# Two normalisation factors spread over the partitions by transfers through memory in place of matmuls

## The chip, the cores and the metric

The kernel runs on one core of one Trainium2 chip. The core has a matrix engine (TensorE, PE in the profile; its weight loads are listed apart as PEld), VectorE (DVE), ScalarE (ACT), GpSimd (POOL) and SyncE (SP), which issues most of the DMA transfers. On-chip data lies in 128 partitions; matmul results go to accumulators in eight banks of their own (PSUM). The metric is the device time of one execution in microseconds, less is better: before the change 732.38 us, the median of three runs (732.17 to 732.54).

## The reference

One block of a hybrid transformer, 512 tokens of width 1024, all in float32. The input is normalised, projected to eleven pieces, and goes through two attention branches whose gated sum is projected back; a squared-ReLU feed-forward layer and a last norm follow.

```python
proj = rmsnorm(h, g_mix) @ w_in
gq, gk, gv, gr, z_gf, z_gb, cq, ckv, kr, z_ma, z_mb = split(proj)
y_gla = gla_branch(gq, gk, gv, gr, z_gf, z_gb, ...)      # gated linear attention, 4 heads
q  = rmsnorm(cq, g_q) @ w_uq                             # latent attention, 8 heads
kv = rmsnorm(ckv, g_kv) @ w_ukv
y_mla = softmax attention of q, k, v with rotary positions
h = h + (sigmoid(z_ma) * y_gla + sigmoid(z_mb) * y_mla) @ w_out
h = h + square(relu(rmsnorm(h, g_mlp) @ w_ff1)) @ w_ff2
return rmsnorm(h, g_final)
```

What matters here is `rmsnorm(cq, g_q)` and `rmsnorm(ckv, g_kv)`: each token's latent (384 features for cq, 256 for ckv) is multiplied by one factor per token, 1 / sqrt(mean of its squares + eps).

## The kernel before

A product in full precision is made of three rounded ones: both operands are split into a rounded part (`h`) and the rest (`l`), and TensorE runs h·h, h·l and l·h into one accumulator (`mm3`). ACT makes the rounded part of a weight, DVE (or POOL) the rest. So one product of 128 features by 512 tokens over the 1024 inputs is 24 matmuls, and its weights pass through DMA (`zb4f`), ACT (`zb4h`) and DVE (`zb4l`) before TensorE can use them.

The program goes through four stretches: the first products with the input (to about 27 us), the big projections gr, za and gv, the four heads of the linear attention (173 to 281 us, with the latents cq and ckv and the gates zb put between as filling), the latent attention with the output projection, and the feed-forward layer.

The projections lie with features on the partitions and tokens along the row. A factor per token is then needed as a row of 512 that is the same in all 128 partitions. The latents' factors begin elsewhere: the sums of squares come out of a matmul with a column of ones (`feature_sums`), which leaves token `p` of block `j` in partition `p`, column `j`, a tile of 128 by 4. Class `Latent` turns these into a row in three steps:

- `sums`: two small DVE instructions and a power on POOL give the factor (`cqr`, `ckvr`).
- `diagonals`: DVE multiplies by `r_x` (the factor of the input's norm), rounds the factor and takes the rest, and multiplies each with the identity, four blocks of 128 by 128 (`cqdg`, `ckvdg`).
- `spread`: two matmuls of a matrix of ones with these diagonals leave the row in all partitions of an accumulator (`cqrs`, `ckvrs`).

`normed` then multiplies the latent's two or three tiles by it on DVE (`cqc`, `ckvc`) and splits them (`cqhl`, `ckvhl`). The up-projections `ro`, `uq`, `uk` and `uv` use the result.

The input's own factor is spread in the same way (`xdg`, `xrs`) in the first stretch. Its squares are summed by ACT from four tiles of the input with tokens on the partitions (`x_rows`, `xr` in the profile).

What sets the order: DVE, ACT, TensorE and POOL run their instructions in the order in which they are written, piece by piece; the part from the last head on is first recorded and then written out by the list `SEQUENCE` (an entry `D:cqc2` is the next DVE instruction that writes a tile cqc2), the last rows by `LAST_ROWS`. A scheduler joins these pieces, and may put the first instructions of the recorded part among the last ones of the part before; it also places the transfers, which SP issues one after the other. `tail`, at the very end, is a row of matmuls of 128 by 64 whose result nobody reads. Tile buffers are taken in turn from pools (26 of the large kind `u4`, four accumulators of the kind `mm`).

Of the kernel before, what the change touches and what calls it, by code (L numbers as in the profile page):

```python
# [11 lines left out]
F32 = mybir.dt.float32  # L12
# [6 lines left out]
P = 128  # L19
S = 512  # L20
# [77 lines left out]
def tile_block(ctx: ExitStack, tc: tile.TileContext, t, out: bass.AP):  # L98
    nc = Held(tc.nc)
    sb = ctx.enter_context(tc.tile_pool(name="sb", bufs=1))  # L100
    pp = ctx.enter_context(tc.tile_pool(name="pp", bufs=4, space=bass.MemoryType.PSUM))

# [200 lines left out]
    def rounded_diagonal(r, name):  # L303
# [3 lines left out]
        return diagonal(rh, rl, name)  # L307

    def diagonal(rh, rl, name):
        diag = u4(f"{name}dg", F32R, (P, 2, NT, P))  # L310
        for x, c in ((0, raw(rh)), (1, rl)):
            nc.vector.tensor_tensor(
                diag[:, x], ident.unsqueeze(1).to_broadcast([P, NT, P]),
                c.unsqueeze(2).to_broadcast([P, NT, P]), op=ALU.mult,
            )
        return diag

    def spread(diag, name, tag="at"):
        rs = ps(tag, f"{name}rs")
        for x in range(2):  # L320
            nc.tensor.matmul(
                rs, ones_r, diag[:, x].rearrange("p a b -> p (a b)"), start=x == 0, stop=x == 1
            )
        return rs
# [172 lines left out]
    x_diag = rounded_diagonal(r_x, "x")  # L497
# [442 lines left out]
    class Latent:  # L940
# [454 lines left out]
    for h in range(GH - 1):  # L1395
# [10 lines left out]
        (rotary.angles, rotary.reduced, cq_.diagonals)[h]()  # L1406
# [49 lines left out]
    ckv_.sums()  # L1456
    zb5 = proj_run(w_b, xT)
# [3 lines left out]
    ckv_.diagonals()  # L1461
# [9 lines left out]
    ckv_.spread()  # L1471
# [394 lines left out]
    def last_rows(ph):  # L1866
# [34 lines left out]
        for _ in range(20):  # L1901
            nc.tensor.matmul(tail[:, : P // 2], ones_r, ones_r[:, : P // 2], start=True, stop=True)
# [106 lines left out]
    for x in range(2):  # L2009
# [4 lines left out]
        S:wr1f P:ckvss*4 D:ckvr D:cqc1 P:kt*4 S:wr1f D:ckvr P:y15*4 A:cqhl1 G:ckvr A:bds P:sc1*5 A:cqhl2 D:sc0 P:y14*4  # L2014
        D:zb4 A:wr0h A:wk0h D:ckvr D:cqhl2 G:wr0l A:wk0h A:qF D:sc1*2 D:cqhl0 A:sc1 S:wk1f D:ckvrh D:ckvdg D:krsin
        D:ckvrl D:ckvdg D:cqhl1 D:sc1 P:zb5*24 A:wr1h D:sc0 A:yg4 D:zb5 G:wr1l A:cos D:kswap A:yg5 G:wk0l S:wq0f
        P:ro0*9 A:kT D:kr P:ckvrs*2 S:wq0f A:wk1h A:wk0h G:wk1l S:wq0f A:sc0 D:roa1 G:qF A:wk0h D:roa0 D:kr P:ro1*9
        G:wk0l D:ckvc0 D:ckvc1 A:ckvhl0 D:ckvhl0 D:kT A:tb5 D:rob1 A:wk1h D:rob0 A:kbuf0 D:roa0 A:ckvhl1 D:kbuf0
        A:wq0h P:zb6*24 A:ro0 D:sc0 G:wq0l D:ro0 G:wk1l S:zb7f P:gla3st*12 A:gla3s D:ckvhl1 G:wk0l P:gla3o1*12 D:roa1
        G:wk0l D:gla3s A:ro1 P:gla3o0*12 D:zb6 S:wq1f D:ro1 S:wq1f S:kbuf1 P:uq0*9 S:q001 S:q000 P:gla3o0*6 A:gla3sq  # L2020
        S:wq1f A:wk1h P:gla3o1*6 A:zb7h S:q000 G:wk1l S:q001 A:gla3sq P:uk0*6 D:zb7l A:gla3sq S:q211 A:q000 S:q110
        A:kbuf0 S:wq2f P:uv01*12 A:kbuf1 D:kbuf0 S:q110 A:gla3sq A:v01 G:gla3ss S:kbuf2 G:gla3ss A:wq1h S:q011 A:wk1h
        G:gla3ss A:q010 G:wq1l S:q010 D:grc D:grb S:q010 D:kbuf1 S:wq2f D:q011 S:w2_10 D:q001 S:wk2f D:grb D:v01
        S:q011 P:zb7*24 D:zb7 S:q211 P:s00*3 D:grc S:q210 P:s01*3 S:w2_20 D:top01 S:w2_30 D:top00 S:wq2f A:e00 P:uq1*9
        A:tb4 P:y17*4 A:q100 P:y16*4 A:e01 P:s03*3 S:q110 D:top03 A:wk2h S:q111 P:s11*3 A:yg6 G:wk2l D:tot00 D:e01
        S:kbuf3 A:e00 G:wk1l D:top11 A:e03 S:q111 P:uk1*6 D:q101 S:bo11f A:kbuf2 P:s02*3 A:wq2h S:q111 A:e11 P:s10*3
        G:wq2l S:bo11f D:top10 S:w2_20 D:top02 A:e10 A:e02 P:uv11*12 P:tp000*4 P:tp001*4 A:wk2h D:tot02 D:kbuf2
        A:pT000 G:wk2l D:tot10 A:tb6 S:kbuf3 D:pT010 P:uv10*12 S:w2_00 A:v10 P:s12*3 A:e02 S:q100 D:top12 A:pT001
        S:q100 D:e03 A:bo11h S:wk3f D:v10 P:uv00*12 S:q101 A:yg7 P:s13*3 P:uq2 D:top13 A:v00 S:kbuf2 A:e10 D:e11
# [12 lines left out]
        A:q300 D:tot40 P:s51*3 P:av2 A:e42 S:q300 D:top51 P:tp310*4 S:q301 D:tb2 A:pT300 S:w2_31 A:e51 D:tot42 D:pT310
        P:uk3*6 S:q311 A:e40 D:e43 S:w2_21 P:s50*3 D:e41 A:q310 G:my1 D:pT311 S:q310 P:tp311*4 A:pT301 P:tp401*4
        D:top50 G:mx1 S:bo20f A:e42 D:pT311 S:w2_31 A:wk3h D:q311 A:kbuf2 G:wk3l A:e50 D:kbuf2 G:yo0 A:pT401 D:tot50
        P:av3*12 D:q301 G:zo1 A:kbuf3 P:tp400*4 D:pT411 G:w2_20 A:pT400 P:tp410*4 A:pT400 P:s61*3 G:w2_11 D:top61
        P:s60*3 G:w2_01 D:top60 A:e61 D:kbuf3 A:e60 P:uv31*12 D:pT410 A:bo50h P:tp411*4 P:av4 D:tb3 A:pT401 P:s62*3
        D:tot60 D:pT410 G:mx1 A:e60 D:top62 G:yo0 D:e51 A:e62 G:my1 P:uv30*12 D:pT411 A:v31 P:s63*3 G:yo1 D:top63
        A:e50 P:s71*3 A:ghyo0 D:e61 G:w2_21 D:top71 A:e63 P:av4*4 G:w2_20 D:bo50l A:e71 P:s70*3 P:tp500*4 A:pT500
        D:tot62 P:tp510*4 S:w2_00 A:v30 D:top70 P:tp600*4 S:h2 A:gao1 D:e63 A:pT500 S:h0 D:pT510 G:gao1 A:pT600 S:h1
        D:v30 P:av4*7 D:pT510 G:yo1 P:wox0*3 D:tb4 P:tp501*4 G:zo0 A:pT501 P:wox1*3 G:glyo0 A:e70 D:pT511 P:s72*3  # L2050
        P:av5 D:pT610 P:tp511*4 G:my2 D:top72 A:pT501 P:s73*3 D:tot70 G:mx2 A:ghyo1 D:pT511 P:av5*2 A:e62 G:zo2 D:e71
        P:tp601*4 A:pT601 G:glyo1 D:v31 A:e72 D:top73 A:e70 P:av5*9 D:pT611 A:e73 P:wox0 P:tp610*4 D:tot72 A:pT600
        D:tb5 P:tp700*4 A:pT700 P:tp701*4 D:pT610 G:my2 P:tp611*4 D:pT710 A:pT601 G:yo2 P:wox1*3 A:e72 D:pT611 G:mx2
# [24 lines left out]
        P:g3x1*12 A:hp2 D:h3 D:hp2 A:junk A:ms2 S:out D:ms2 S:out D:ms3 D:hp3 P:gend*14 P:tail*20 A:junk D:ms3 A:hp3  # L2078
# [122 lines left out]
```

## Time and profile before

| | |
|---|---|
| median of three runs | 732.38 us (732.17 to 732.54) |
| the profiled execution: its time, and its span from the first to the last instruction | 732.09 us, 730.3 us |
| TensorE busy, matmuls | 726.3 us (99%), 4174 |
| DVE, ACT, POOL busy | 619.8 (85%), 498.7 (68%), 225.8 us (31%) |
| TensorE clock granted, mean | 0.999 |
| the four matmuls cqrs and ckvrs | at 241.5 and 265.1 us |

A row of a timeline is: start in us, length in us, engine, line, operation, output <- inputs, the sizes and how many; in brackets what the engine idled for just before, in us. Nearly all instructions have one of two lines: L76 where a list writes them out, L90 elsewhere. The letters f, h and l at the end of a weight's name are its full, rounded and rest copy; numbers of buffers are left out. A matmul's length is the time until its result is out; the next one starts earlier, so that 24 matmuls of 512 columns take about 5.44 us.

### The profile page before, as it was taken

The page shows a single profiled execution, that of the slowest core. Times are in us where ns is not written, and L with a number is a line of the kernel's source. Part 1 is how long each engine was busy: PE and PEld are TensorE (multiplying, and loading weights), DVE is VectorE, ACT ScalarE, POOL GpSimd, SP SyncE. Part 2 cuts the span into 40 slices and gives each one's busy share as a digit, 9 for nine tenths or more (in the row PEclk, how much of TensorE's full clock was granted, in tenths as well). Part 3 has the DMA queues.
Part 4 walks back from the last instruction along what each step waited for, and adds up shares of the span by engine and source line. Part 5 has one row for each costly group of instructions (what it writes and reads, how often), then busy time and mean ns, then how long its engine had stood idle before and what let it go on. Part 6 is the DMA issues. An engine that isn't in the chain of part 4 may idle for free.

```text
span 730.3 us, 11455 instructions
## 1 busy us (share of the span) xinstructions
PE 726.3 (99%) x4174; PEld 641.2 (88%) x4174; DVE 619.8 (85%) x859; ACT 498.7 (68%) x846; POOL 225.8 (31%) x290
## 2 busy tenths in 40 slices
PE   9999999999999999999999999999999999999998
PEld 8888888888888888888888999889988998899987
DVE  6677887889988897789999789998699869987797
ACT  7456565595696864988866889545774477646976
POOL 1842020243843843226763512200111012100224
PEclk9999999999999999999999999999999999999999
DMA  9968683521222324657957899871987088814864
GB/s 323 346 176 198 210 180 88 84 62 29 58 58 59 89 46 110 184 158 189 251 88 208 196 205 201 187 215 57 245 182 201 9 223 206 206 59 134 183 89 143
DMA packets 82777, 112.06 MB, mean 153 GB/s; under 512 B 16384, under 2 KB 35712, under 8 KB 82720
## 3 DMA queue, kind: packets, MB, share of 16 engines
q1 hardware_dynamic: 65344, 77.81, 34.0%
q0 software_dynamic: 17088, 33.30, 27.3%
q8 instruction: 33, 0.54, 0.3%
q10 hardware_dynamic: 288, 0.22, 0.1%
q14 instruction: 24, 0.20, 0.1%
HBM read 106.32 MB, written 2.10 MB: 148 GB/s over the span
## 4 chain that ended last, share of the span: by engine, by line
PE 99%; issue 0%
PE f3x L90 3%; PE f2x L90 3%; PE f1x L90 3%; PE f0x L90 3%; PE first L90 3%; PE s L76 3%; PE av L76 3%; PE wox L76 3%; PE g2x L90 3%; PE g1x L90 3%; PE g0x L90 3%; PE gvx L90 3%; PE zax L90 3%; PE grx L90 3%; PE gk L90 2%; PE cq L90 2%
## 5 line engine op out<-in xcount | busy, mean ns | idle before, releaser
L90 POOL DMA_DIRECT2D w<-in_w_ff x32 | 38.6, 1205 | 240.1 <-DMA w<-in_w_ff 134.8
L76 ACT ACTIVATE e<-s,top 128x512 f32<-128x512 f32 x32 | 21.9, 688 | 8.5 <-DVE top L76 7.4
L76 DVE TENSOR_REDUCE top<-s 128x1 f32<-128x512 f32 x32 | 21.6, 682 | 5.8 <-PE s L76 5.6
L76 PE MATMUL s<-kbuf,q 96*128 96x512 f32 x96 | 26.3, 400 | 0.0
L76 PE MATMUL av<-pT,v 128*128 128x512 f32 (+1 forms) x108 | 25.2, 371 | 0.0
L76 DVE TENSOR_TENSOR pT<-tp,pT 128x512 fp32r<-128x512 f32 x32 | 21.7, 683 | 2.4 <-ACT pT L76 1.0
L76 ACT ACTIVATE pT<-tp 128x512 fp32r<-128x512 f32 x32 | 18.5, 596 | 6.1 <-PE tp L76 5.9
L76 PEld LDWEIGHTS av<-pT,v 128*128 128x128 f32 x108 | 18.6, 188 | 3.3
L76 PEld LDWEIGHTS s<-kbuf,q 96*128 96x128 f32 x96 | 17.2, 189 | 3.3 <-DVE grb L76 0.2
L76 PE MATMUL tp<-ident,e 128*128 128x128 f32 x128 | 17.1, 272 | 0.0
L76 PEld LDWEIGHTS tp<-ident,e 128*128 128x128 f32 x128 | 15.0, 141 | 2.2 <-ACT e L76 0.2
L90 POOL DMA_DIRECT2D gvw<-in_w_in x4 | 4.8, 1226 | 38.7 <-DVE gvw L90 34.0
L90 POOL TENSOR_TENSOR qF<-qk,qF 128x512 fp32r<-128x512 f32 x3 | 5.3, 1761 | 32.8 <-ACT qF L90 32.8
L90 POOL DMA_DIRECT2D zaw<-in_w_in x4 | 4.8, 1216 | 32.4 <-DVE zaw L90 27.7
L76 POOL DMA_DIRECT2D w<-in_w_ff x8 | 10.0, 1354 | 15.1 <-DVE g360l L76 7.1
L90 DVE TENSOR_TENSOR w<-w,w 128x1024 f32<-128x1024 f32 x12 | 14.4, 1220 | 0.1
L90 ACT ACT_TABLE_LOAD x9 | 11.5, 1283 | 1.2 <-PEq L2171 0.8
L76 POOL DMA_DIRECT2D w<-in_w_out x10 | 12.2, 1452 | 0.0
L76 ACT ACTIVATE e<-e,tot 128x512 f32<-128x512 f32 x16 | 11.3, 720 | 0.0
L76 POOL TENSOR_TENSOR my<-tb,yg 128x256 f32<-128x256 f32 x8 | 6.2, 772 | 15.6 <-DVE tb L76 9.4
L90 ACT ACTIVATE f1h<-f1a 128x512 fp32r<-128x512 f32 x10 | 6.1, 621 | 6.2 <-DVE f1a L90 6.2
L90 ACT ACTIVATE f2h<-f2a 128x512 fp32r<-128x512 f32 x10 | 6.1, 620 | 6.2 <-DVE f2a L90 6.2
(1975 smaller groups left out, 3099.7 us busy)
## 6 DMA issues: line engine op xcount, KB each, us to landing
w<-in_w_ff SPq DMA_DIRECT2D x48, 512.0 KB, 5.7
w<-in_w_ff POOLq DMA_DIRECT2D x40, 512.0 KB, 6.2
w<-in_w_out POOLq DMA_DIRECT2D x10, 512.0 KB, 6.1
grw<-in_w_in SPq DMA_DIRECT2D x8, 512.0 KB, 9.0
zaw<-in_w_in SPq DMA_DIRECT2D x8, 512.0 KB, 6.3
gvw<-in_w_in SPq DMA_DIRECT2D x8, 512.0 KB, 4.9
w<-in_w_out SPq DMA_DIRECT2D x16, 256.0 KB, 3.8
w221f<-in_w_ff SPq DMA_DIRECT2D x8, 512.0 KB, 5.0
```

The source lines that it names most:

```text
L76: what(*args, **options)
L90: return what(*args, **options)
```

## The change

The row of factors is no longer made by matmuls. POOL multiplies the factor by `r_x`; one transfer stores the tile of 128 by 4 as a row of 512 numbers in a tensor in device memory; a second, which waits for it, loads that row into all 128 partitions of an on-chip tile. `diagonals` is gone. The spread of the input's factor keeps its matmuls. Two edits keep it company: the rows of x are loaded in four transfers instead of eight, and `tail` has 24 matmuls instead of 20.

```diff
+    hbm = ctx.enter_context(tc.tile_pool(name="hbm", bufs=1, space=bass.MemoryType.DRAM))
...
-        for c in range(2):
-            cols = slice(c * S, (c + 1) * S)
-            nc.sync.dma_start(x_rows[i][:, cols], t["x"][0, i * P : (i + 1) * P, cols])
+        nc.sync.dma_start(x_rows[i], t["x"][0, i * P : (i + 1) * P, :])
...
-        def diagonals(self):
-            nc.vector.tensor_tensor(self.r, self.r, r_x, op=ALU.mult)
-            self.diag = rounded_diagonal(self.r, self.name)
-
         def spread(self):
-            self.rs = spread(self.diag, self.name, "mm")
+            nc.gpsimd.tensor_tensor(self.r, self.r, r_x, op=ALU.mult)
+            row = hbm.tile([S], F32, tag=f"{self.name}row", name=f"{self.name}row")
+            self.rs = u4(f"{self.name}rs", F32, (P, S))
+            nc.sync.dma_start(row.rearrange("(a p) -> p a", p=P), self.r)
+            nc.sync.dma_start(self.rs, row.partition_broadcast(P))
...
-        (rotary.angles, rotary.reduced, cq_.diagonals)[h]()
+        if h < 2:
+            (rotary.angles, rotary.reduced)[h]()
...
                 ckv_.begin(0)
                 cq_.sums()
+                cq_.spread()
...
-            cq_.spread()
...
     ckv_.sums()
+    ckv_.spread()
...
-    ckv_.diagonals()
...
-    ckv_.spread()
...
-        for _ in range(20):
+        for _ in range(24):
```

In `SEQUENCE` the entries `D:ckvr` (the third), `D:ckvrh`, `D:ckvrl`, both `D:ckvdg` and `P:ckvrs*2` go, `G:ckvr` becomes `G:ckvr*2`, and `S:ckvrow` and `S:ckvrs` come in.

**DVE, third head of the linear attention, before.** cqr is the factor, cqdg the diagonals, rrf the running sums of the forward gate, cqc a latent tile; the product with cqrs stands further down, behind the four qkf and qkb:

```order
L90 TENSOR_SCALAR mb_2270<-gateb_2267,gvec 128x512
L90 TENSOR_TENSOR cqr_2190<-cqr_2190,r_x 128x4
L90 CAST cqrh_2305<-cqr_2190 128x4
L90 TENSOR_TENSOR cqrl_2306<-cqr_2190,cqrh_2305 128x4
L90 TENSOR_TENSOR cqdg_2309<-ident,cqrh_2305 128x512
L90 TENSOR_TENSOR cqdg_2309<-ident,cqrl_2306 128x512
L90 SCALAR_TENSOR_TENSOR rrf_2312<-mf_2265,l_2261 128x128 x4
...
L90 TENSOR_TENSOR qkb_2258<-gkn_421_2218,eeb_2361 128x512
L76 TENSOR_TENSOR cqc_388_2025<-cqc_388_2025,cqrs_2475 128x512
L90 TENSOR_TENSOR zb4l_2459<-zb4f_2456,zb4h_2458 128x1024
```

The same place in the changed program:

```order
L90 TENSOR_SCALAR mb_2273<-gateb_2270,gvec 128x512
L76 TENSOR_TENSOR cqc_388_2023<-cqc_388_2023,cqrs_2194 128x512
L90 SCALAR_TENSOR_TENSOR rrf_2307<-mf_2268,l_2264 128x128 x4
...
L90 TENSOR_TENSOR qkb_2261<-gkn_422_2221,eeb_2356 128x512
L90 TENSOR_TENSOR zb4l_2454<-zb4f_2451,zb4h_2453 128x1024
```

Five instructions are gone, and the first product with cqrs has moved from behind qkb to ahead of rrf, where it waits for the second transfer.

**SP, the queue of transfers around both rows, before** (zb4f to zb7f, wr, wk and wq are weights in full precision, w the first output weights):

```order
L90 DMA zb4f_2456<-in_w_in 128x8x128
L90 DMA zb5f_2507<-in_w_in 128x8x128
L76 DMA w_11_797_2848<-in_w_out 128x512
...
L76 DMA wr1f_2565<-in_w_uq 128x8x16 x3
L76 DMA wk1f_2627<-in_w_ukv 128x2x384
L76 DMA wq0f_2594<-in_w_uq 128x2x64 x3
```

The same places now:

```order
L90 DMA zb4f_2451<-in_w_in 128x8x128
L90 DMA zb5f_2499<-in_w_in 128x8x128
L90 DMA cqrow<-cqr_2188 128x4x1
L90 DMA cqrs_2194<-cqrow 128x512
L76 DMA w_11_791_2838<-in_w_out 128x512
...
L76 DMA wr1f_2556<-in_w_uq 128x8x16 x3
L76 DMA ckvrow<-ckvr_2540 128x4x1
L76 DMA wk1f_2617<-in_w_ukv 128x2x384
L76 DMA ckvrs_2542<-ckvrow 128x512
L76 DMA wq0f_2584<-in_w_uq 128x2x64 x3
```

The store and the load of cq's row stand together behind zb5f; those of ckv's row have wk1f between them. On PE the two pairs of matmuls are simply gone, from between gla2o and ckv and from between the two ro products.

More of the change, by code (lines that the diff above doesn't have):

```diff
@@ L301, in feature_sums, with diagonal @@
         return tot
-    def rounded_diagonal(r, name):
+    def diagonal(r, name):
         rh, rl = sm(f"{name}rh", dt=F32R), sm(f"{name}rl")
@@ L306, in rounded_diagonal @@
         nc.vector.tensor_tensor(rl, r, raw(rh), op=ALU.subtract)
-        return diagonal(rh, rl, name)
-    def diagonal(rh, rl, name):
         diag = u4(f"{name}dg", F32R, (P, 2, NT, P))
@@ L496, in tile_block @@
     first_with(7)
-    x_diag = rounded_diagonal(r_x, "x")
+    x_diag = diagonal(r_x, "x")
     for _, lows in zb_early:
@@ L2013, in tile_block @@
         S:w2_11 S:zb6f S:w2_01 S:wr0f*2 A:sin A:zb6h D:cqc2 S:wk0f D:zb6l S:wr0f P:bd*4 D:cqc0 S:wr1f P:sc0*5 A:cqhl0
[L2014 to L2017, printed above, removed]
@@ L2053, in tile_block @@
-        D:tb5 P:tp700*4 A:pT700 P:tp701*4 D:pT610 G:my2 P:tp611*4 D:pT710 A:pT601 G:yo2 P:wox1*3 A:e72 D:pT611 G:mx2
+        S:wr1f P:ckvss*4 D:ckvr D:cqc1 P:kt*4 S:wr1f D:ckvr P:y15*4 A:cqhl1 G:ckvr*2 S:ckvrow A:bds P:sc1*5 A:cqhl2
+        D:sc0 P:y14*4 D:zb4 A:wr0h A:wk0h D:cqhl2 G:wr0l A:wk0h A:qF D:sc1*2 D:cqhl0 A:sc1 S:wk1f S:ckvrs D:krsin
+        D:cqhl1 D:sc1 P:zb5*24 A:wr1h D:sc0 A:yg4 D:zb5 G:wr1l A:cos D:kswap A:yg5 G:wk0l S:wq0f P:ro0*9 A:kT D:kr
+        S:wq0f A:wk1h A:wk0h G:wk1l S:wq0f A:sc0 D:roa1 G:qF A:wk0h D:roa0 D:kr P:ro1*9 G:wk0l D:ckvc0 D:ckvc1
@@ L2054, in tile_block @@
+        P:tp700*4 A:pT700 P:tp701*4 D:pT610 G:my2 P:tp611*4 D:pT710 A:pT601 G:yo2 P:wox1*3 A:e72 D:pT611 G:mx2
         P:woz1*3 A:bo20h P:wox0*2 G:zo0 P:av6 A:bo21h D:bo20l G:yo2 P:av7*5 A:gdo2 A:pT701 D:e73 A:gao2 G:zo1 D:pT711
@@ L2077, in tile_block @@
         G:ms2 P:g3x1*3 A:gend D:ms0 S:out*2 A:ms1 S:out*2 D:h3 G:ms3 A:junk P:g3x0*12 S:out G:hp3 D:h2 D:hend A:junk
-        P:g3x1*12 A:hp2 D:h3 D:hp2 A:junk A:ms2 S:out D:ms2 S:out D:ms3 D:hp3 P:gend*14 P:tail*20 A:junk D:ms3 A:hp3
+        P:g3x1*12 A:hp2 D:h3 D:hp2 A:junk A:ms2 S:out D:ms2 S:out D:ms3 D:hp3 P:gend*14 P:tail*24 A:junk D:ms3 A:hp3
         D:hp3 D:ms3 A:ms3 S:out A:out
```

70 lines of the change are left out of this document (35 added, 35 removed).

## The prediction

> **What bounds the kernel now.** I read the page's busy shares and chain first, then the chain in order of time around the two places where the changed matmuls stand, then what the weight loads of TensorE wait for, then the timelines of VectorE (DVE), ScalarE (ACT), GpSimd (POOL) and the DMA queue there.
>
> ```profile
> PE 726.3 (99%) x4174; PEld 641.2 (88%) x4174; DVE 619.8 (85%) x859; ACT 498.7 (68%) x846; POOL 225.8 (31%) x290
> PE 99%; issue 0%
> ...
> 241.66 0.46 PE cqrs L90 x2
> ...
> 247.58 5.46 PE zb L90 x24
> ...
> 263.17 2.11 PE ro L76 x9
> 265.28 0.47 PE ckvrs L76 x2
> 265.75 2.09 PE ro L76 x9
> ```
>
> The first two lines are the page's, the others the chain in order of time (start, length, what). TensorE is the bound: the chain never leaves it. The four matmuls that go are in it, 0.46 us (cqrs) and 0.47 us (ckvrs): 0.93 us at most, 0.13% of the time. So the question is whether TensorE can run ahead by that much or then meets data that isn't there yet. The list of what weight loads wait for is short; of its entries these two lie next to the second pair:
>
> ```profile
> PEld ro L76 <- DVE cqhl L76: 0.2, 1, 0.2
> PEld ro L76 <- DVE zb L76: 0.2, 1, 0.2
> ```
>
> A tighter place is not in that list, because it is only 0.08 us. The weight loads from 247 us (start, length), and the work on DVE and ACT that makes zb4l, the low halves of the next weights:
>
> ```profile
> 246.51 0.41 PEld L90 LDWEIGHTS ckv<-xT,ckv1h 128*128 128x128 f32 x2
> 246.97 0.19 PEld L90 LDWEIGHTS ckv<-xT,ckv1l 128*128 128x128 f32 x1
> 247.19 0.41 PEld L90 LDWEIGHTS zb<-xT,zb4h 128*128 128x128 f32 x2
> 247.73 0.19 PEld L90 LDWEIGHTS zb<-xT,zb4l 128*128 128x128 f32 x1
> ```
>
> ```profile
> 235.17 1.37 DVE L90 TENSOR_TENSOR_SCAN rrf<-mf,l 128x128 f32<-128x128 f32 x4 [0.83 <-ACT l L90]
> ...
> 246.45 1.23 DVE L90 TENSOR_TENSOR zb4l<-zb4f,zb4h 128x1024 fp32r<-128x1024 f32 x1 [1.87 <-ACT zb4h L90]
> ```
>
> ```profile
> 241.61 1.16 ACT L90 ACTIVATE eeb<-difb 128x512 f32<-128x512 f32 x2 [0.17 <-DVE difb L90]
> ...
> 245.34 1.08 ACT L90 ACTIVATE zb4h<-zb4f 128x1024 fp32r<-128x1024 f32 x1
> ```
>
> In ckv the low load comes 0.46 us after the high ones (246.51 to 246.97); in zb4 0.54 us after. DVE ends zb4l at 246.45 + 1.23 = 247.68, and the load starts at 247.73: **zb4l is exactly just in time.** It hangs on no TensorE work after 241 us: ACT makes zb4h at the end of a gapless run that starts at 241.61 with eeb, eeb waits for DVE's difb, and DVE has worked without a gap from rrf at 235.17, which waited for ACT's l.
>
> **The change part by part.**
>
> First pair (cqrs). TensorE comes to ckv and zb4 0.46 us earlier, would load zb4l at 247.73 - 0.08 - 0.46 = 247.19, and it is ready at 247.68 as before. It waits the 0.46 us there: −0.46 and +0.46, **0**. Unless the run from rrf to zb4l moves, and there the new wait enters. The first product with cqrs on DVE stood behind qkb; in the changed program it stands ahead of rrf and waits for the second transfer:
>
> ```profile
> 231.93 0.74 DVE L90 TENSOR_SCALAR mb<-gateb,gvec 128x512 f32<-128x512 f32 x1
> ...
> 243.91 0.67 DVE L76 TENSOR_TENSOR cqc<-cqc,cqrs 128x512 f32<-128x512 f32 x1
> ```
>
> DVE is free at 231.93 + 0.74 = 232.67 (the five instructions of the diagonal that filled the gap are gone), and rrf can't start before 235.17. The product takes 0.67 us, so the row must have landed by 234.50. Each us later delays rrf, difb, eeb, zb4h and zb4l, all in order, and with zb4l TensorE, by 1 us. When does it land? The chain: POOL's power, POOL's new product with r_x (priced by the same product for gla1ss), the store of the row, the load to all partitions.
>
> ```profile
> 221.65 0.20 POOL L90 TENSOR_TENSOR gla1ss<-gla1ss,r_x 128x4 f32<-128x4 f32 x1
> ...
> 226.09 1.01 POOL L90 TENSOR_TENSOR cqr<-cqr,mhalf 128x4 f32<-128x4 f32 x1 [1.44 <-DVE cqr L90]
> ```
>
> ```profile
> 225.76 0.37 SPq L90 DMA_DIRECT2D zb5f<-in_w_in  x1
> ```
>
> ```profile
> zb5f<-in_w_in SPq DMA_DIRECT2D x1, 512.0 KB, 5.9
> ...
> wr0f<-in_w_uq SPq DMA_DIRECT2D x3, 64.0 KB, 3.4
> wq0f<-in_w_uq SPq DMA_DIRECT2D x3, 64.0 KB, 2.1
> ...
> w<-in_w_out SPq DMA_DIRECT2D x4, 256.0 KB, 2.9
> w<-in_w_out SPq DMA_DIRECT2D x16, 256.0 KB, 3.8
> ```
>
> ```profile
> 230.50:231.00 0.50, 0.50 (x3) 0.40 (x3) 0.50 (x2) 0.50 (x3) 0.00 (x0) 1.00 0.13 29
> ```
>
> The factor is ready at 226.09 + 1.01 + 0.20 = 227.30, and SP is free then. The last figure of a DMA row is the time from issue to landing. The store is 2 KB in 512 pieces of 4 bytes. wr0f moves 64 KB in 1024 pieces of 64 bytes, wq0f the same in 256 pieces: 1.3 us for 768 pieces, so 512 pieces cost some 0.87 us. The load is 256 KB in rows of 2 KB, like w: 2.9 us in the stretch 236 to 292 us, 3.8 over the whole kernel.
> - Early end: store 2.1, load 2.9: landed 232.3, 2.2 us to spare, no delay.
> - Late end on this queue: the store is issued 1.5 us behind zb5f, on the same queue, and zb5f lands only at 225.76 + 5.9 = 231.66; the row of the stretch 230.5 to 231 us (last two figures: DMA share 0.13, 29 GB/s) shows a few late pieces of it still moving. Held behind them the store lands at 231.66 + 0.87 = 232.53. With a load of 2.9 us the row lands at 235.4, the product ends at 236.1: rrf 0.9 us late. With 3.8 us: 1.8 us late.
> - Below nothing it can't go, since rrf waits for ACT's l in any case.
>
> The share of 0.13 is two of the 16 DMA engines. Whether they are late again I can't decide, so I take the middle of not held (0) and held (0.9): **+0.5 us**. The rival below has the far end.
>
> [...]
>
> Second pair (ckvrs). TensorE is limited by DVE at both ro products (the two entries of waits above), and DVE loses work just ahead:
>
> ```profile
> 262.53 0.69 DVE L76 TENSOR_TENSOR ckvdg<-ident,ckvrl 128x512 fp32r<-128x512 f32 x1
> 263.14 0.68 DVE L76 TENSOR_TENSOR cqhl<-cqc,cqhl 128x512 fp32r<-128x512 f32 x1
> ...
> 268.92 1.28 DVE L76 TENSOR_TENSOR ckvc<-ckvc,ckvrs 128x512 f32<-128x512 f32 x2
> ```
>
> Without the two ckvdg (the second is shown; the first is its like) cqhl is done over 1.3 us earlier, so its wait goes, and the accumulator of the second ro then no longer waits for DVE's zb product (it gets another bank). Nine matmuls at zb's pace take 9 x 5.46 / 24 = 2.05 us; the two ro took 2.11 and 2.09: 0.06 and 0.04 back. Behind them nothing hangs on work from before 265 us but ckvc, which now waits for the second row:
>
> ```profile
> 256.47 1.01 POOL L76 TENSOR_TENSOR ckvr<-ckvr,mhalf 128x4 f32<-128x4 f32 x1 [3.32 <-DVE ckvr L76]
> ```
>
> ```profile
> 259.96 0.37 SPq L76 DMA_DIRECT2D wk1f<-in_w_ukv  x1
> ```
>
> Ready at 257.7; the store behind three transfers like wr0f, 3.4 us: 261.1; wk1f is issued between them, at 259.96, as before; the load, 3.8 us beside it: 264.9. ckvc starts at 268.92, or some 1.5 us earlier with DVE lighter: over 2 us of cover, and TensorE has a whole zb product (5.4 us) and the last head's state to do before it needs what comes of it. So **−0.47 − 0.10 = −0.57 us**, and what follows is paced by TensorE and moves along.
>
> Tail and rows of x.
>
> ```profile
> 725.01 2.15 PE tail L76 x20
> 726.79 0.35 ACTq L76 DMA_DIRECT2D out<-ms  x1
> ...
> out<-ms ACTq DMA_DIRECT2D x1, 192.0 KB, 2.6
> ```
>
> ```profile
> 25.72 1.75 DVE L90 TENSOR_TENSOR zb2l<-zb2f,zb2h 128x1024 fp32r<-128x1024 f32 x1
> 27.86 0.40 PE L90 MATMUL zb<-xT,zb2l 128*128 128x512 f32 x1
> ```
>
> Four more tail matmuls, 4 x 2.15 / 20 = 0.43 us, end at 727.6; the last store, issued at 726.79, lands 2.6 us later, at 729.4, and covers them; uncovered they would cost 0.43. The rows of x come as four transfers of 512 KB in place of eight of 256, the same bytes in the same order; DVE has 27.86 - 27.47 = 0.39 us to spare at zb2l, the first place that depends on them. I take 0, between −0.1 and +0.3.
>
> Sum against the profiled execution (span 730.3, time 732.09): 0 + 0.5 − 0.57 = −0.1. The median of the runs shown, 732.38, is 0.29 above that execution; the same difference from there gives **732.3 us**.
>
> **Rivals.**
> - *The whole gain arrives.* zb4l turns out not to bind (DVE or ACT run it earlier) and the row is on time: −0.46 − 0.57 = −1.03, 731.4. For it: the wait there today is 0.08 us and in no list. Against: the run from rrf to zb4l has no gap that the change shortens. Chance 0.12. Even this is 0.14%; only with a gain in the first stage as well does it pass 0.2%.
> - *The row comes far too late.* The load of one 2 KB row to 128 partitions, or the store in 4-byte pieces, is much dearer than the rows above. A transfer of the kernel that spreads a row so is gfin, on POOL's queue:
>
> ```profile
> w<-in_w_ff POOLq DMA_DIRECT2D x40, 512.0 KB, 6.2
> ...
> gfin<-in_g_final POOLq DMA_DIRECT2D x1, 512.0 KB, 6.3
> ```
>
> With 6.3 us for the load behind a held store the product ends at 232.53 + 6.3 + 0.67 = 239.5: rrf 4.3 us late, 4.3 − 0.57 = +3.7, 736.1. It decides from a landing after 236.5, where the loss passes the 0.57 won back by 1.46 us. Against it: w on the same queue takes 6.2 us for as many bytes without a spread, so the spread itself cost nothing there. [...] Chance 0.13.
> - *Nothing is gained at the second pair either.* ckvrs comes after ckvc is due, or the next thing that is just in time holds TensorE: +0.5 alone, 732.9. For it: DVE is 85% busy. Against: the 2 us of cover. Chance 0.13.
>
> **How the numbers follow.** Forecast 0.62, rivals 0.12, 0.13 and 0.13. The forecast's own range is 731.8 (row on time) to 733.6 (1.8 us late); downwards the first rival belongs in it, of the second only the start: 731.2 to 733.7. A measurement of this kernel tells about 0.2%, 1.46 us, from no change. Faster by more than that would need 730.9: 0.08, the first rival with luck in the first stage. Slower: 0.13, the second. Else no difference: 0.79.
>
> **What would show it.** In the changed profile: no cqrs and ckvrs on PE; an entry of zb waiting for DVE zb4l of some 0.4 us; DVE's first cqc waiting for the DMA of cqrs, and rrf at 235.2 to 236.1; the two ro entries gone from the waits of PEld; ckvc not waiting for a DMA; the last stores 0 to 0.6 us earlier. I am wrong if the zb load does not wait, if cqrs lands before 232 or after 236.5, or if the first stage of TensorE has a gap.

## The result, and the profile after

The change made the kernel **slower: 744.65 us** (median of five, 744.09 to 745.0) against 732.17 us of the kernel before on the same chip (731.63 to 732.54, five). The ratio is 1.017, its 95% interval 1.0156 to 1.0185. The profiled execution took 744.19 us with a span of 742.4, so the span grew by 12.1 us.

From the page of the changed kernel: busy time, granted clock by slices, share of the chain.

```profile
PE 730.6 (98%) x4174; PEld 644.9 (87%) x4174; DVE 617.4 (83%) x849; ACT 498.7 (67%) x846; POOL 223.8 (30%) x292
...
PEclk9999999999999998999999999999999999999999
...
PE 86%; DVE 6%; DMA 4%; POOL 1%; ACT 1%; issue 1%; DVEq 0%; ACTq 0%; POOLq 0%; SPq 0%
```

TensorE was 99% of the chain before and is 86% now. There are just as many matmuls, yet its busy time rose from 726.3 to 730.6 us, and in one slice the granted clock is below 0.9. The chain in order of time (start, length, what) names the new links:

```profile
227.31 8.10 DMA cqrow<-cqr
...
235.47 4.71 DMA cqrs<-cqrow
...
263.00 11.29 DMA ckvrow<-ckvr
...
274.31 4.52 DMA ckvrs<-ckvrow
```

The two stores of 2 KB take 8.10 and 11.29 us, far longer than the loads of 256 KB behind them. What this does to DVE, in its timeline (in brackets the idle time just before):

```profile
240.21 0.69 DVE L76 TENSOR_TENSOR cqc<-cqc,cqrs 128x512 f32<-128x512 f32 x1 [7.62 <-DMA cqrs<-cqrow]
240.82 1.36 DVE L90 TENSOR_TENSOR_SCAN rrf<-mf,l 128x128 f32<-128x128 f32 x4
...
278.86 2.55 DVE L76 TENSOR_TENSOR ckvc<-ckvc,ckvrs 128x512 f32<-128x512 f32 x2 [5.63 <-DMA ckvrs<-ckvrow]
```

The row for cq is there at 240.18, not by 234.50, and rrf starts 5.65 us later than before (235.17). The row for ckv is there at 278.83. The list of TensorE's waits (in total, times, longest); gla2o and gla3st are matmuls of the third and the fourth head of the linear attention:

```profile
PE gla3st L76 <- DVE kT L76: 4.6, 1, 4.6
PE gla2o L90 <- DVE gla2s L90: 3.3, 1, 3.3
...
PE zb L90 <- DVE zb4l L90: 0.3, 1, 0.3
```

That is 8.2 us of waiting; less the 0.93 us of the removed matmuls it leaves nearly 5 us of the 12.1 unexplained. They are in the granted clock behind each of the two long waits. The table by stretches of 1 us has the busy times of PE, PEld, DVE, ACT and POOL, then the granted clock, the DMA share and GB/s:

```profile
244.00:245.00 1.00, 1.00 (x8) 1.00 (x7) 1.00 (x3) 1.00 (x4) 0.00 (x0) 0.68 0.00 0
245.00:246.00 1.00, 1.00 (x6) 0.90 (x5) 0.93 (x3) 0.26 (x1) 0.01 (x1) 0.50 0.14 23
246.00:247.00 1.00, 1.00 (x4) 0.81 (x3) 0.97 (x2) 0.24 (x1) 1.00 (x3) 0.50 0.75 186
247.00:248.00 1.00, 1.00 (x4) 0.77 (x4) 1.00 (x3) 1.00 (x4) 1.00 (x3) 0.61 1.11 339
...
281.00:282.00 1.00, 0.00 (x0) 0.00 (x0) 1.00 (x3) 1.00 (x1) 0.00 (x0) 0.95 0.00 0
282.00:283.00 1.00, 0.34 (x1) 0.34 (x2) 1.00 (x3) 0.99 (x3) 0.00 (x0) 0.50 0.00 0
...
288.00:289.00 1.00, 1.00 (x7) 1.00 (x7) 1.00 (x2) 0.24 (x1) 1.00 (x2) 0.63 1.02 306
```

Busy time multiplied by what is missing to 1.00, row by row: 0.32 + 0.50 + 0.50 + 0.39 = 1.71 us behind the first wait; 0.17 + 5 x 0.50 + 0.37 = 3.04 us behind the second (283 to 288 is 0.50 throughout). The sum 8.2 + 4.75 − 0.93 = 12.0 us stands against the 12.1 measured. **So in this execution the two late rows stand for 8 us of waiting and, behind the waits, almost 5 us of half-speed matmuls.** That the sum closes does not yet say that the run without the half speed would be 5 us shorter; the run `filled` below asks that.

### The profile page after: what moved, and what is told of

Read it like the earlier page. It is cut to its first block, busy times and chain, and to the rows that moved or that the text cites. A ratio compares the mean times of both kernels' runs of the same rounds, so it can differ in the third digit from the quotient of the medians.

```text
span 742.4 us, 11446 instructions
## 1 busy us (share of the span) xinstructions
PE 730.6 (98%) x4174; PEld 644.9 (87%) x4174; DVE 617.4 (83%) x849; ACT 498.7 (67%) x846; POOL 223.8 (30%) x292
## 4 chain that ended last, share of the span: by engine, by line
PE 86%; DVE 6%; DMA 4%; POOL 1%; ACT 1%; issue 1%; DVEq 0%; ACTq 0%; POOLq 0%; SPq 0%
PE f3x L90 3%; PE f2x L90 3%; PE f1x L90 3%; PE f0x L90 3%; PE first L90 3%; PE s L76 3%; PE av L76 3%; PE wox L76 3%; PE g2x L90 3%; PE g1x L90 3%; PE g0x L90 3%; PE gvx L90 3%; PE zax L90 3%; PE grx L90 3%; PE zb L90 2%; PE g3x L76 2%
## 5 line engine op out<-in xcount | busy, mean ns | idle before, releaser
L76 PEld LDWEIGHTS s<-kbuf,q 96*128 96x128 f32 x96 | 17.2, 189 | 3.3 <-DVE grb L76 0.2
L90 ACT ACT_TABLE_LOAD x9 | 11.5, 1283 | 1.2 <-PEq L2167 0.8
L76 POOL DMA_DIRECT2D w<-in_w_out x10 | 12.2, 1449 | 0.0
L76 ACT ACTIVATE e<-e,tot 128x512 f32<-128x512 f32 x16 | 11.3, 720 | 0.0
```

The lines of the kernel that those rows point to most:

```text
L76: what(*args, **options)
L90: return what(*args, **options)
```

## The experiments

### Which part costs what

*One row alone.* In `cq_only` only the cq row goes through memory; ckv keeps its diagonal and matmuls. `ckv_only` is the reverse. Both load x in four transfers and have a tail of 22.

```diff
 # cq_only, against the kernel before
-        (rotary.angles, rotary.reduced, cq_.diagonals)[h]()
+        if h < 2:
+            (rotary.angles, rotary.reduced)[h]()
...
+                cq_.spread()
...
-            cq_.spread()
...
-    ckv_.spread()
+    ckv_.products_spread()
 # ckv_only, against the change
-        if h < 2:
-            (rotary.angles, rotary.reduced)[h]()
+        (rotary.angles, rotary.reduced, cq_.diagonals)[h]()
...
-                cq_.spread()
...
+            cq_.products_spread()
```

In both, `spread` goes through memory and `products_spread` makes the row by the two matmuls, as `spread` did before.

> The first row through memory, the second by matmuls as before (tail 22, x in 4 transfers). My theory is that each part costs its own waits and, after them, a stretch of halved TensorE clock: the 3.5 us wait at gla2o stays, zb4l stays 0.7 us late, some 3.3 us of matmuls at clock 0.5 behind the gap cost 1.65, and the removed pair gives back 0.46, so 732.2 + 3.5 + 0.7 + 1.65 - 0.46 = 737.6 us, with the clock back at 1.00 by 250 us. Rival 1, the clock falls only because two gaps follow each other: no halved stretch here, 735.9. Rival 2, the loss is made at the second row alone and the first wait is given back later: 732 to 733.

> The second row through memory, the first by matmuls as before. My theory: the wait of 4.8 us at gla3st stays, some 5.7 us of matmuls at clock 0.5 behind it cost 2.85, the removed pair gives 0.47 back, so 732.2 + 4.8 + 2.85 - 0.47 = 739.4 us; with the run that has only the first row the two differences add up to the 12.5 us of the whole change within 0.6. Rival 1, no clock loss after a single gap: 736.5. Rival 2, the second row is late only because the first one has delayed the transfers ahead of it on SP's queue: the store takes 3 to 5 us, no wait at gla3st, 731.7 to 732.7.

Measured: `cq_only` 739.03 us (738.8 to 739.32, ratio 1.0095, 1.008 to 1.011), `ckv_only` 737.54 us (737.37 to 739.43, ratio 1.008, 1.0066 to 1.0094), against 732.17. The differences, 6.86 and 5.37, add up to 12.2 of the 12.5 us. Each part loses alone, so the second row is not late because of the first. The figures were missed by 1.4 and 1.9 us, in opposite directions. One part of that is the clock. `cq_only` by stretches:

```profile
243.00:244.00 1.00, 0.00 (x0) 0.00 (x0) 0.97 (x4) 0.00 (x0) 0.61 (x1) 0.89 0.00 0
...
250.00:251.00 1.00, 1.00 (x4) 0.77 (x4) 0.27 (x1) 1.00 (x6) 0.92 (x4) 0.69 0.03 10
```

and `ckv_only`:

```profile
276.00:277.00 1.00, 0.00 (x0) 0.00 (x0) 1.00 (x3) 0.99 (x2) 0.00 (x0) 0.99 0.00 0
...
280.00:281.00 1.00, 1.00 (x9) 1.00 (x8) 1.00 (x2) 0.57 (x2) 1.00 (x2) 0.80 0.00 0
```

With 0.50 between the two rows, the half clock lasts from 243.78 to 250.62, 6.84 us, in the one and from 276.98 to 280.40, 3.42 us, in the other. In the change itself, by the rows above, it is 244.36 to 247.78 (3.42) and 281.90 to 288.74 (6.84): one unit of 3.42 us or two, and which of them a gap gets changed from kernel to kernel.

Worked out as above, the half speed costs 1.5 us in `ckv_only` where 2.85 was expected, and the wait in the list of weight loads is 4.6 us in place of 4.8; that is most of the miss there. In `cq_only` it costs 3.0 where 1.65 was expected, but the row is also later than in the change (the store takes 8.9 us, the load 5.3), so the wait at gla2o is 4.9 us in place of 3.5, and the 0.7 us at zb4l is gone. The mean clocks of the single executions hint at what a unit is worth: in `cq_only` two of them have 0.994 and 0.995 (738.98 and 739.32 us) and two 0.997 (739.08 and 738.80), which take no less; in `ckv_only` the one with 0.995 takes 739.43 us and the three with 0.997 take 737.37 to 737.58. A second unit would then cost nothing that shows behind the first gap and some 1.9 us behind the second. Only one execution of each has a profile, so this is not shown.

*x's rows alone.* The kernel before with four transfers of x.

```diff
-        for c in range(2):
-            cols = slice(c * S, (c + 1) * S)
-            nc.sync.dma_start(x_rows[i][:, cols], t["x"][0, i * P : (i + 1) * P, cols])
+        nc.sync.dma_start(x_rows[i], t["x"][0, i * P : (i + 1) * P, :])
```

> The kernel before with x's rows in 4 transfers instead of 8 and nothing else of the change. All theories put nothing on it: 732.2 with a difference of at most 0.3 us, first TensorE product of the stages behind the start at the same time within 0.1 us.

Measured: 732.54 us (732.16 to 733.15, 11 runs) against 732.17; ratio 1.0005, 0.9997 to 1.0014. No difference that can be told, though the median lies 0.07 us beyond the expected bound, and in the one profile TensorE waits 0.5 us for zb2l, where the kernel before has no such wait. The first matmul with zb2l starts at 27.87 against 27.86 us, the next one with zb2h at 28.20 against 28.09.

### What makes the store slow

*16-byte pieces.* Everything as in the change, but a partition's four factors are stored side by side, and DVE reads the row with a step.

```diff
-            nc.sync.dma_start(row.rearrange("(a p) -> p a", p=P), self.r)
+            nc.sync.dma_start(row.rearrange("(p a) -> p a", p=P), self.r)
...
-                nc.vector.tensor_tensor(c, c, self.rs, op=ALU.mult)
+                by_token = lambda x, order: x.rearrange(order, p=P)
+                c4 = by_token(c, "q (a p) -> q a p")
+                nc.vector.tensor_tensor(c4, c4, by_token(self.rs, "q (p a) -> q a p"), op=ALU.mult)
```

> The change, but each partition's four factors are stored side by side (128 pieces of 16 bytes instead of 512 of 4) and VectorE reads the spread row with a step of 16 bytes; nothing else moves. Theory A, the 512 scattered pieces make the store's time: it falls from 8.1 and 11.3 us to 2 to 3.5, rows land near 235 and 265 to 268, no TensorE wait over 1 us at gla2o or gla3st, clock 1.00 throughout, 731.3 to 733.5 us. Theory B, the time is the queue's (a 512 KB load ahead of the first store, many small pieces ahead of the second, both on SP's queue): stores stay at 7 to 11 us and the run at 743 to 745. Between: the store falls with the number of pieces only in part (4 to 6 us), one row still late, 735 to 740.

Measured: **732.46 us** (732.1 to 733.06, ten runs), ratio 1.0004, 0.9995 to 1.0013. The 12.5 us are gone. The page's list of DMA issues (the last figure is the time to landing):

```profile
cqrow<-cqr SPq DMA_DIRECT2D x1, 2.0 KB, 3.5
ckvrow<-ckvr SPq DMA_DIRECT2D x1, 2.0 KB, 3.6
```

Same queue, same transfers ahead of them, same 2 KB: 3.5 and 3.6 us where 8.1 and 11.3 stood. The granted clock is 1.000. The layout of the store is the whole loss; what it is about the layout is left open by this run (a quarter of the pieces, and each four times as large).

*Number, size, queue or place.* Stores that nothing reads, added to the kernel before in a quiet stretch, of a tile of 128 by 4.

```diff
+    nc.sync.dma_start(probe("n512b4")[0:S].rearrange("(a p) -> p a", p=P), r_x)     # and six more
...
+    nc.scalar.dma_start(by_act.rearrange("(a p) -> p a", p=P), r_x)
+    nc.gpsimd.dma_start(by_pool.rearrange("(a p) -> p a", p=P), r_x)
```

> The kernel before, with seven extra stores of r_x (128x4) or of one row to a scratch tensor in memory from 113 us on, SP's queue otherwise empty, each waiting for the one ahead of it, and two more stores of 512 pieces issued by ACT and by POOL around 180 us; nothing reads them. Theory A, the number of 4-byte pieces makes the time: 512 pieces take 6 to 9 us alone as behind a 512 KB load, and on ACT's queue as on SP's; 128 pieces of 16 or of 4 bytes 2 to 3.5; 256 of 8 bytes 4 to 6; the same 512 pieces set 64 bytes apart as long as side by side; one piece of 2 KB about 2. Theory B, the queue's load makes it: 512 pieces take 2 to 3.5 us alone, and only the first, issued behind a 512 KB load, takes 7 or more. Theory C, neighbouring pieces wait for one another in memory: 64 bytes apart they take less than half as long as side by side.

The seven on SP's queue did not wait for one another as meant: they were issued within 4.2 us (113.20 to 117.37) and say nothing one by one. The other two do. ACT's store, alone on its queue while SP loads 512 KB, and POOL's:

```profile
by_act<-r_x ACTq DMA_DIRECT2D x1, 2.0 KB, 9.1
by_pool<-r_x POOLq DMA_DIRECT2D x1, 2.0 KB, 10.1
```

So theory B falls: the time is not that of SP's queue. All times of this and the next two runs are of one execution each. The next run held the stores apart with a load of one word behind each:

```diff
+    piece = hbm.tile([n], F32, tag=name, name=name)
+    nc.sync.dma_start(to(piece), src)
+    nc.sync.dma_start(back[:, 0:1], piece[0:1].rearrange("(p a) -> p a", p=1))   # waits for the store
```

> The kernel before, with seven stores to scratch tensors from 113 us on, now one after the other: behind each stands a load of its first word, so that SP's queue issues the next store only when the one ahead has landed. Theory, the time goes with the number of pieces, by a fixed part and some 12 to 20 ns a piece (from 3.5 us for 128 and 8.1 to 11.3 for 512 in place): 512 of 4 bytes 8 us, 128 of 16 bytes 3.3, 256 of 8 bytes 4.5 to 5.5, 128 of 4 bytes 3.3, 1024 of 4 bytes 14 to 20, 512 of 4 bytes set 64 bytes apart 8, one piece of 2 KB about 2. Rival, size decides, not number: 128 of 4 bytes take as long as 512, or 256 of 8 bytes no longer than 128 of 16. Rival, neighbours wait for one another: 64 bytes apart takes half or less.

```profile
pa<-r_x SPq DMA_DIRECT2D x1, 2.0 KB, 11.0
...
pb<-r_x SPq DMA_DIRECT2D x1, 2.0 KB, 2.5
...
pd<-r_x SPq DMA_DIRECT2D x1, 0.5 KB, 7.9
...
pe<-R SPq DMA_DIRECT2D x1, 4.0 KB, 17.2
...
pf<-r_x SPq DMA_DIRECT2D x1, 2.0 KB, 1.9
```

pa is the change's layout, pb 128 pieces of 16 bytes, pd 128 of 4 bytes side by side, pe 1024 of 4 bytes, pf 512 of 4 bytes set 64 bytes apart. For the other two, pc and pg, no landing is listed, but the load behind each is issued only when the store has landed (11.06 us behind pa, which landed after 11.0):

```profile
127.88 0.37 SPq L90 DMA_DIRECT2D pc<-r_x  x1
130.88 0.23 SPq L90 DMA_DIRECT2D back<-pc  x1
```

So pc, 256 pieces of 8 bytes side by side, takes at most 3.0 us (4.5 to 5.5 expected), and pg, 2 KB in one piece, at most 1.2 (159.12 to 160.31). My theory of number fell: 128 adjacent words take 7.9 us (some of that beside POOL's loads), and 512 words that stand apart take **1.9**. The rival of neighbours held for pieces of 4 bytes; pieces of 8 bytes are quick though they too lie side by side. The next run made the distance the question, with the same 512 words at several distances:

```diff
+    for name, w in (("qa", 16), ("qb", 1), ("qc", 2), ("qd", 4), ("qe", 8)):     # w words apart
+        store(name, w * S, every(w), r_x)
+    store("qf", 4 * P, every(4), r_x[:, 0:1])
+    store("qg", P, every(1), r_x[:, 0:1])
```

> As the stores one after the other before, to tell number from nearness: 512 pieces of 4 bytes set 64 bytes apart first (behind a 512 KB load), then 4, 8, 16 and 32 bytes apart, then 128 pieces 16 and 4 bytes apart; each alone on SP's queue. Theory, pieces of 4 bytes in one 64-byte line wait for one another: 64 bytes apart 2 to 4 us in spite of the load ahead, 4 bytes apart 8 to 11 us, and between them a time that falls as the pieces in a line fall from 16 to 2 (32 apart 2 to 3, 16 apart 3 to 5, 8 apart 5 to 7); 128 pieces 4 bytes apart 8 again, 16 apart 2 to 4. Rival, the long times came from other traffic at those moments: the first store is now the long one (8 to 11 us) and 4 bytes apart takes 2 to 3. Rival, only the 4-byte step is slow (two 4-byte pieces in 8 bytes): 8 apart takes 2 to 3 like the others.

```profile
qa<-r_x SPq DMA_DIRECT2D x1, 2.0 KB, 5.0
qb<-r_x SPq DMA_DIRECT2D x1, 2.0 KB, 9.4
qc<-r_x SPq DMA_DIRECT2D x1, 2.0 KB, 4.2
qd<-r_x SPq DMA_DIRECT2D x1, 2.0 KB, 2.9
qe<-r_x SPq DMA_DIRECT2D x1, 2.0 KB, 4.8
qf<-r_x SPq DMA_DIRECT2D x1, 0.5 KB, 3.4
qg<-r_x SPq DMA_DIRECT2D x1, 0.5 KB, 11.5
```

| pieces of 4 bytes, distance of their starts | 512 pieces | 128 pieces |
|---|---|---|
| 4 bytes (side by side) | 9.4 alone, 11.0 behind a 512 KB load | 7.9, 11.5 * |
| 8 bytes | 4.2 | |
| 16 bytes | 2.9 | 3.4 * |
| 32 bytes | 4.8 * | |
| 64 bytes | 1.9 alone, 5.0 behind a 512 KB load | |

(* beside POOL's loads of 512 KB, which start at 134.54 us.) Words side by side are dear wherever they are issued from (9.1 us by ACT, 10.1 by POOL, 9.4 by SP); at twice the distance less than half is left (4.2), at four times a third (2.9; both less than expected). That the words wait for one another in memory was my reading of these times; no trace shows the wait. A load ahead in the queue is not nothing, 3.1 us from 1.9 to 5.0, but it does not make 8 or 11. The rival of other traffic falls with qb: 9.4 us while nothing else is on the DMA engines (0 to 1 GB/s), where qa, behind the load, took 5.0. At which distance the price ends was not found: it falls step by step, 9.4, 4.2 and 2.9 us at 4, 8 and 16 bytes, and qe is disturbed.

### What the late row does

*The first product put back.* The change's stores, but DVE's first product with the cq row is bound to come behind `zb4_rest`, the instruction that writes zb4l; it now stands behind zb5l.

```diff
     in_program_order(written)
+    issued_after([i for i in nc.cur_bb.bb.instructions[written:] if i.engine == mybir.EngineType.DVE][0], zb4_rest)
```

> The change with its scattered stores, but VectorE's first product with the cq row is put behind the last weights of the stage (zb4l and zb5l), in place of ahead of rrf. Theory: the first row then lands at 240 us as in the change, some 10 us before it is read, so the waits at gla2o (3.5) and zb4l (0.7) and the clock loss behind them go, and the 0.46 us pair is gained; the second row stays as late as where it is changed alone: 737.5 - 0.46 = 737.1 us, 736.8 to 737.8. Rival: the 8 us in which SP's queue stands for the store costs by itself (the loads w and zb6f behind it): waits appear at the matmuls of those tiles and the run stays above 739.

Measured: 737.81 us (736.99 to 739.14, four runs), ratio 1.0079, 1.0066 to 1.0093.

```profile
cqrow<-cqr SPq DMA_DIRECT2D x1, 2.0 KB, 8.8
```

The wait at gla2o is gone although the store takes as long; the wait at gla3st stays, 4.8 us in the list of weight loads. The time falls by 6.8 us, as much as `cq_only` loses. So the first row's loss is made by the place of that one product on DVE, and SP's standing for the store costs nothing that can be seen. The median, 0.01 us above the upper edge of what was expected, is that of `ckv_only` (737.54) within its spread: the 0.46 us of the first pair, which the expectation counted, are not won (below). The runs spread over 2.2 us; that the half clock lasts one unit in some and two in others would explain it. The slowest has a mean clock of 0.995 and two units in its profile, the others 0.996 and 0.997, but they have no profile, so this is only argued.

*The gaps filled.* Idle matmuls in front of gla2o and gla3st keep TensorE at work while it would wait.

```diff
+        for _ in range(20 if h == 3 else 0):
+            nc.tensor.matmul(acc, ones_r, xT[0][:, 0, :], start=True, stop=True)
...
+        for _ in range(14 if h == 2 else 0):
+            nc.tensor.matmul(accs[0], ones_r, xT[0][:, 0, :], start=True, stop=True)
```

> The change with 14 idle matmuls of 128x512 (3.2 us) ahead of gla2o and 20 (4.6 us) ahead of gla3st, written to the accumulator that the first real matmul clears; they fill the two gaps in which TensorE waits and compute nothing of the result. Theory, the clock falls because TensorE stands idle for 3 to 5 us: waits as in the change (what is late is still late, within 0.4 us), granted clock 1.00 throughout, 744.65 - 1.65 - 2.87 = 740.1 us. Rival, the clock falls for another reason (the DMA burst, the dense work after the gap): the clock still drops to 0.5 at 244 and 282, and the run stays at 744 to 745.

Measured: 743.33 us (741.98 to 743.68, four runs), ratio 1.015, 1.0136 to 1.0163. The clock stays at 1.00 through both places; a row in each:

```profile
244.00:246.00 2.00, 2.00 (x13) 1.71 (x12) 1.90 (x6) 0.50 (x2) 0.87 (x3) 1.00 0.37 80
...
284.00:286.00 2.00, 1.78 (x15) 1.57 (x14) 1.94 (x4) 1.68 (x4) 1.25 (x2) 1.00 0.00 0
```

That the clock falls because TensorE stands idle is shown. That it costs 4.75 us is not: by the medians only 1.3 us came back, with intervals that overlap. The list of what weight loads wait for has the reason:

```profile
PEld zb L90 <- ACT zb4h L90: 1.2, 1, 1.2
PEld zb L90 <- DVE zb4l L90: 1.0, 1, 1.0
PEld gla3st L76 <- DVE kT L76: 0.8, 1, 0.8
...
PEld gla3o L76 <- DVE sc L76: 0.4, 1, 0.4
PEld s L76 <- DMA q<-ro: 0.4, 1, 0.4
```

At half speed TensorE had waited 0.7 us for zb4's weights; at full speed it waits 2.2. The 34 idle matmuls at 5.46 / 24 us each, 7.7 us, and these five waits, 3.8, make 11.5 us; the same list for the change has 3.5 at gla2o, 0.7 at zb4l and 4.8 at gla3st, 9.0. So 2.5 of the 4.75 us went to waits for work that was late anyway: more than half of the half-speed time had been hidden in them. What is left, 2.2 us, is the difference of the two profiled executions (744.19 and 741.98); the profiled one of `filled` is its fastest.

### What the change is worth with a quick store

*Both remedies,* 16-byte pieces and the first product put back; then the same with x in eight transfers and a tail of 20, as before the change; then, also, ScalarE makes zb4h before gla2o's squares.

```diff
 # contig_late: the diffs of contiguous and late_product together
 # contig_late_8: and
-        for _ in range(24):      # tail; x_rows in four
+        for _ in range(20):      # tail; x_rows in eight
 # early_zb4: and
+        if h == 2:
+            zb = begin(C_ZB + 4 * P, "zb4")
...
         rs = gla_squares(h, os)
...
-            zb = begin(C_ZB + 4 * P, "zb4")
```

> Both remedies: stores of 16 bytes a partition and the first product behind zb5l. Theory: no TensorE wait is left at gla2o, zb or gla3st, both pairs' 0.93 us are gained in the stages from 225 to 290 us, 732.17 - 0.93 = 731.2 us before what the start and the end of the run give back (731.2 to 732.0; contiguous stores alone, with zb4l 0.7 us late, gave 732.46). Rival: another step of the same stages takes up the gain, as it did before the change when zb4l was just in time: 732.3 to 732.7.

> Both remedies, with x's rows in 8 transfers and the tail of 20 matmuls as before, so that only the two rows and the first product's place differ from the kernel before. Theory: as with both remedies alone, since the x transfers and the tail weigh nothing: 731.2 to 732.0 us, 731.6 likeliest. Rival, the 4 transfers or the tail of 24 had cost some 0.3 us: 731.0 to 731.4.

> Both remedies with x's rows and the tail as before, and ScalarE makes zb4h ahead of the four squares of gla2o in place of behind them (1.4 us earlier), so zb4l is ready about 246.1 us, a us before TensorE loads it. Theory, it was zb4l that took up the first pair's gain: the wait of 0.57 us at the load of zb4l goes, the zb product starts some 0.45 us earlier, and the time falls from 0.38 to about 0.8 us below the kernel before (ratio 0.9989). Rival, the squares, now 1.1 us later, hold up POOL's gla2ss and with it grb, grc and zb5l on VectorE, and TensorE waits at zb5 or ro for what it no longer waits for at zb4: the time stays at 0.4 us below, ratio 0.9994 to 0.9998, with a new entry of waits.

| | median (runs) | before, same chip | ratio, interval |
|---|---|---|---|
| contig_late | 731.73 (11) | 732.15 | 0.9997, 0.9988 to 1.0006 |
| contig_late_8 | 731.99 (11) | 732.37 | 0.9998, 0.9989 to 1.0007 |
| early_zb4 | 731.97 (11) | 732.03 | 0.9998, 0.9989 to 1.0007 |

None can be told from the kernel before. The first two lie in their expected range, the second at its upper end; `early_zb4` is 0.06 us below the kernel before, where its theory had 0.38 to 0.8 and its rival 0.4. The traces tell more than the times. `contig_late_8`, chain in order of time, and its weight loads of zb4:

```profile
226.06 0.89 PE bd L90 x8
...
257.77 5.47 PE zb L76 x24
...
272.76 1.43 PE gla3st L76 x12
```

```profile
247.62 0.19 PEld L90 LDWEIGHTS zb<-xT,zb4l 128*128 128x128 f32 x1 [0.57 <-DVE zb4l L90]
```

The chain of the kernel before has, at the same places:

```profile
226.17 0.89 PE bd L90 x8
...
257.70 5.48 PE zb L76 x24
...
273.28 1.43 PE gla3st L76 x12
```

There zb4l was loaded at 247.73. I count from bd, matmuls ahead of both places, since the profiles differ by some tenths of a us up to there. From the start of bd to the load of zb4l it is 21.56 us in both: the first pair's 0.46 us is taken up whole by a wait of 0.57. From zb5's product to gla3st it is 14.99 us against 15.58: the second pair brings 0.59. From bd to gla3st, though, only 0.41 us is won (46.70 against 47.11): between the two places the matmuls sc wait 0.2 us for DVE's ckvr, for which they did not wait before. In `early_zb4`, chain and waits:

```profile
225.94 0.89 PE bd L90 x8
...
257.39 5.50 PE zb L76 x24
```

```profile
PEld sc L76 <- DVE ckvr L76: 0.4, 1, 0.4
```

The wait at zb4l is gone, as meant. From bd, zb5's product begins after 31.45 us, against 31.71 in `contig_late_8` and 31.53 before: 0.26 of the 0.45 expected, because the matmuls sc now wait 0.4 us for DVE's ckvr. Further on the scores s wait 0.3 us for a transfer. Neither pure theory nor pure rival, then: the wait at zb4l did take the first pair's gain, and when it was gone, part of the gain met what was just in time next. With intervals of 0.18% more can't be said. A version that beats the kernel before by a measurable amount was not found.

## Why the prediction was wrong, step by step

- **TensorE bounds the kernel, and 0.93 us is all there is to gain**: nothing speaks against it. With a quick store and the product put back, the medians lie 0.06 to 0.42 us below the kernel before, with intervals that all include no change.
- **First pair, 0, because zb4l is exactly just in time**: right: 21.56 us from bd to zb4l's load with the pair and, in `contig_late_8`, without it.
- **The new wait: DVE's first product ahead of rrf, deadline 234.50, each us later costs 1 us**: the mechanism is right. `late_product` takes that place away, and the loss of the first row goes with it. In the change rrf is 5.65 us late and zb4l is loaded at 252.88 instead of 247.73, 5.15 us. `contiguous` shows the same at the size that was forecast: its row lands at 234.81, DVE's product then takes 1.10 us, rrf starts 9.28 us behind bd against 9.16 before, and zb4l is loaded 21.84 us behind bd against 21.72 (bd's first matmul at 226.57 and 226.01). The 0.12 us late at rrf is 0.12 us at zb4l.
- **The store: 2.1 us and 0.87 us for its 512 pieces**: *this is the step that failed.* It measured 8.10, and at the second row, where I had put 3.4, 11.29. I took the price of a piece from loads in pieces of 64 and 256 bytes (wr0f and wq0f), as if a piece cost the same whatever its size, its direction and its neighbours. A store of adjacent words is another thing: 9.4 us with nothing beside it, and 1.9 when the same words stand 64 bytes apart. The bounds taken from these rows were no bounds, since no row was near: before the change this kernel has no row of words stored one by one. The load was mis-sized too, by less: 4.71 and 4.52 us against the 2.9 to 3.8 assumed.
- **Held behind zb5f**: there is such a cost (1.9 to 5.0 us for the words that stand apart), but it was not the one that decided.
- **Second pair, −0.57**: 0.59 with a quick store. In the change the row landed at 278.83, not at 264.9, 13.9 us late against "over 2 us of cover".
- **Not in the sum at all: the clock.** I let a late row cost what it is late. Each of the five stops of 3.3 to 4.7 us in the profiles was followed by 3.42 or 6.84 us at half clock (0.50 granted). From the last matmul ahead of the stop to the drop it was 3.0 us (`late_product`) to 4.1 (the change, first stop). No row of the kernel before shows such a stretch. This price belonged in the rival.
- **Tail and rows of x, 0**: `rows_only` can't be told from no change, nor can `contig_late` from `contig_late_8`.
- **The rival that the row comes far too late** is what happened, with 0.13. Its place and its point of decision (a landing after 236.5; it was 240.18) were right. Its price, 736.1, came from a dear load; the store was what was dear, the second row was late as well, and the clock was missing. What was dear is words side by side: the added stores of 512 of them took 9.1 to 11.0 us, from SP, ACT and POOL. It is not the small piece as such, for 512 words set 64 bytes apart took 1.9 us, nor the size of the transfer, for the same 2 KB in 128 pieces of 16 bytes took 2.5. The sign named for being wrong, cqrs landing after 236.5, is the row that showed it.

## What to carry to other kernels

Price a transfer by a row of the same kind: direction, size of a piece, and how near the pieces lie in memory; where the profile has none, the range must say so instead of borrowing from loads. When 2 KB leave a tile of 128 by 4, store what lies together in a partition together, and let the reader take the stride: here the two stores took 3.5 and 3.6 us in place of 8.1 and 11.3. The step costs the reader time too (last point below). And a wait on TensorE as long as those here, 3.3 us or more, is priced with the half-speed stretch behind it (3.42 or 6.84 us at 0.50 here), less whatever would have been late there anyway; a product that waits for a new transfer belongs behind the work that the next stage needs (6.8 us here, in `late_product`).

## What the runs showed of the hardware that I had not expected

- Stores of 4-byte words side by side in device memory were slow: 9.4 us for 512 of them, 7.9 and 11.5 for only 128, 17.2 for 1024 (these three beside other loads), against 1.9 for 512 that stand 64 bytes apart and at most 3.0 for 256 pieces of 8 bytes side by side. Issuing from ACT's or POOL's queue didn't help (9.1 and 10.1).
- A transfer behind such a store on the same queue was slow with it: wk1f, 384 KB, took 12.5 us where it took 3.4 before and 3.7 with 16-byte pieces.
- In the profiles the half clock lasted one or two units of 3.42 us: one behind gaps of 3.3 (the change) and 4.4 us (`ckv_only`), two behind gaps of 4.6 (the change, `late_product`) and 4.7 (`cq_only`). Whether the length of the gap decides is not shown. The drop did not always fall into the gap: in the change TensorE was at work again from 243.56 and the clock fell at 244.36.
- DVE was slower reading the row with a step of 16 bytes: the three cqc products of `contiguous` took 1.07 to 1.10 us, with POOL idle, against 0.68 to 0.69 with the plain row in the change. A plain one took 1.10 once too (in `late_product`, while POOL ran a product), so the step is not the only thing that slows it. The first of them lies on the path of `contiguous`: rrf starts behind it.
